# A 4096 x 4096 x 4096 matmul with leaky ReLU: casts, evictions and stores dealt out anew to the engines

## The chip, the cores and the metric

The kernel runs on one core of a Trainium2 chip. The metric is the device time of one execution in microseconds (us). The program is one launch; inputs and output lie in the chip's main memory (DRAM) in float32.

Engines as the profile names them: PE (TensorE, the matmuls), PEld (its weight loads), DVE (VectorE), ACT (ScalarE), POOL (GpSimd), SP (SyncE, which here only issues DMAs). An entry like ACTq or SPq is the part of an engine that issues DMAs and waits.

## What is computed

```python
a: (4096, 4096) float32     # m, k
b: (4096, 4096) float32     # k, n
alpha = 0.01
x = a @ b
out = where(x > 0, x, alpha * x)      # (4096, 4096) float32
```

Both inputs are random normal numbers. The kernel rounds a and b to bfloat16 and accumulates in float32.

## The kernel before, in words

**Tiles.** K is cut into `KU` = 4 units of 1024 (`KC` = 8 slices of 128). M is cut into `MB` = 4 blocks of 1024 rows, each with two halves (`h`) of 512 rows, that is `MT` = 4 row blocks (`mt`) of 128. N is cut into 4 column blocks of `RN` = 1024, that is `NP` = 2 pieces (`nt`) of 512. A *region* is one half of a block of rows times one column block: 512 x 1024 of the output. It fills all eight PSUM banks (4 row blocks x 2 pieces of 512 columns) and takes 4 units x 64 = 256 matmuls of 128 x 512. There are 32 regions (8192 matmuls), in this order: block of rows, column block (forwards in even blocks, backwards in odd ones), half. Two neighbouring regions share B (a *pair*), and at a change of the block of rows B stays as well, so there are 13 different pairs of B loads.

**A.** `load_a` (line 67) fetches a row block's 128 rows x 1024 k in four DMAs of SyncE (32 partitions each, runs of 1 KB, quarters in the order 0, 2, 1, 3) into one of four `a32` buffers, rounds them to bfloat16 on VectorE (line 74, a strided cast) and transposes 32 x 32 blocks on VectorE (line 76) into `at`. There are 10 `at` buffers, for 8 units in use.

**B.** `load_b` (line 81) fetches 128 x 1024 (512 KB) in one DMA of SyncE into one of four `b32` buffers and rounds it on ScalarE (line 84) into `bt`. There are 5 `bt` buffers of one unit.

**Order of the work.** The program is written out by hand (`manual_schedule`): each engine runs its instructions in the order in which the Python code issues them, and waits only by semaphores for data and for free buffers. `jobs` (lines 98 to 112) attaches the loads to units: a pair's B one region ahead, a new block's A two regions and a unit ahead. A unit's loads are issued before its matmuls (line 169). So all casts of a region's units stand on ScalarE ahead of that region's evictions.

**Start.** `first_unit` loads A's four row blocks and B's eight slices of one unit in the order `ababbabbabbb`. In region 0, the units 0 to 2 run their matmuls in the order in which those pieces arrive; unit 3, and all units of the later regions, run row block by row block (`mt`, then c, then `nt`). Region 1's A is loaded at the end of region 0.

**End of a region.** In unit 3, after each row block, ScalarE empties its two banks (line 196, leaky ReLU into an `o` tile of 128 x 512, four buffers) and issues the two stores itself (line 201, 256 KB each). The next region's first matmul on a bank waits for that.

Of the kernel before, what the change touches and what calls it, by code (L numbers as in the profile page):

```python
# [7 lines left out]
P = 128  # L8
BF16 = mybir.dt.bfloat16
FP32 = mybir.dt.float32  # L10
KC = 8
NT = 512
MT = 4
NP = 2


@with_exitstack
def kernel(
    ctx: ExitStack,
    tc: tile.TileContext,  # L20
    a: bass.AP,
    b: bass.AP,
    alpha,
    out: bass.AP,
):

    nc = tc.nc
    M, K = a.shape
    K2, N = b.shape
# [9 lines left out]
    QW = KC * P // 4  # L45

    a_v = a.rearrange("(mt g i) (u q w) -> mt u q i g w", g=4, i=32, q=4, w=QW)
    b_v = b.rearrange("(u p c) n -> u p c n", u=KU, p=P, c=KC)
# [12 lines left out]
    at = {}  # L61
    bt = {}

    def new_a(mb, h, u):
        at[mb, h, u] = at_pool.tile([P, KC, RM], BF16, name="at")

    def load_a(mb, h, u, mt):

        tile_no = (mb * HALVES + h) * MT + mt
        a32 = a32_pool.tile([P, 4, QW], FP32, name="a32")  # L70
        for q in (0, 2, 1, 3):
            nc.sync.dma_start(a32[32 * q:32 * q + 32], a_v[tile_no, u, q])  # L72
        a16 = a16_pool.tile([P, 4, KC, 32], BF16, name="a16")
        nc.vector.tensor_copy(a16, a32.rearrange("p g (j c) -> p g c j", c=KC))  # L74
        dst = at[mb, h, u][:, :, mt * P:(mt + 1) * P].rearrange("p c (g i) -> p g c i", g=4)
        nc.vector.transpose(dst, a16)  # L76

    def new_b(pair, n, u):
        bt[pair, u] = bt_pool.tile([P, KC, RN], BF16, name="bt")

    def load_b(pair, n, u, c):
        b32 = b32_pool.tile([P, RN], FP32, name="b32")
        nc.sync.dma_start(b32, b_v[u, :, c, n * RN:(n + 1) * RN])  # L83
        nc.scalar.copy(bt[pair, u][:, c, :], b32)  # L84


    regions = []
    pairs = []
    for mb in range(MB):
        order = list(range(NB)) if mb % 2 == 0 else list(range(NB - 1, -1, -1))  # L90
        for n in order:
# [6 lines left out]
    jobs = {}  # L98
    for s_region, (mb, h, pi, n) in enumerate(regions):
        if h:  # L100
            continue
        for u in range(KU):
            if regions[s_region - 1][2] != pi or s_region == 0:
                s = s_region * KU + u
                jobs.setdefault(max(0, s - KU), []).append(("b", pi, n, u, s))
            if s_region and regions[s_region - 1][0] != mb:
                for hh in range(HALVES):
                    idx = hh * KU + u
                    s = s_region * KU + idx
                    jobs.setdefault(s - HALVES * KU - 1, []).append(("a", mb, hh, u, s))  # L110

    jobs = {s: [j for j in v if not (j[0] == "b" and j[1] == 0)] for s, v in jobs.items()}

    def run(job):
        if job[0] == "a":
            _, mb, h, u, _ = job
            new_a(mb, h, u)
            for mt in range(MT):
                load_a(mb, h, u, mt)
        else:  # L120
            _, pi, n, u, _ = job
            new_b(pi, n, u)
            for c in range(KC):
                load_b(pi, n, u, c)


    w = warm_pool.tile([P, NT], BF16, name="w")
    nc.vector.memset(w, 0.0)  # L128
    wp = psum_pool.tile([P, NT], FP32, name="ps")
    for i in range(9):  # L130
        nc.tensor.matmul(wp, w[:, :P], w, start=True, stop=True)  # L131

    def first_unit(u):
        new_a(0, 0, u)
        new_b(0, 0, u)
        for what in "ababbabbabbb":
            if what == "a":
                load_a(0, 0, u, first_unit.a)
                first_unit.a += 1
            else:  # L140
                load_b(0, 0, u, first_unit.b)
                first_unit.b += 1
        first_unit.a = first_unit.b = 0

    first_unit.a = first_unit.b = 0

    def mm(ps, mb, h, pi, u, mt, nt, c):
        nc.tensor.matmul(  # L148
            ps,
            at[mb, h, u][:, c, mt * P:(mt + 1) * P],  # L150
            bt[pi, u][:, c, nt * NT:(nt + 1) * NT],
            start=(u == 0 and c == 0),
            stop=(u == KU - 1 and c == KC - 1),
        )

    first_unit(0)
    for r, (mb, h, pi, n) in enumerate(regions):
        banks = {}
        for u in range(KU):
            s = r * KU + u  # L160
            if r == 0:
                if u + 1 < KU:
                    first_unit(u + 1)
                else:
                    for uu in range(KU):
                        new_a(0, 1, uu)
                        for mt in range(MT):
                            load_a(0, 1, uu, mt)
            for job in jobs.get(s, []):
                run(job)  # L170
            if u == 0:
                for mt in range(MT):
                    for nt in range(NP):
                        banks[mt, nt] = psum_pool.tile([P, NT], FP32, name="ps")
            if r == 0 and u < KU - 1:

                na = nb = 0
                for what in "ababbabbabbb":
                    if what == "a":
                        todo = [(na, c) for c in range(nb)]  # L180
                        na += 1
                    else:
                        todo = [(mt, nb) for mt in range(na)]
                        nb += 1
                    for mt, c in todo:
                        for nt in range(NP):
                            mm(banks[mt, nt], mb, h, pi, u, mt, nt, c)
                continue
            for mt in range(MT):
                for c in range(KC):  # L190
                    for nt in range(NP):
                        mm(banks[mt, nt], mb, h, pi, u, mt, nt, c)
                if u == KU - 1:
                    for nt in range(NP):
                        o = o_pool.tile([P, NT], FP32, name="o")
                        nc.scalar.activation(  # L196
                            o, banks[mt, nt], mybir.ActivationFunctionType.Lrelu, alpha=alpha
                        )
                        row = ((mb * HALVES + h) * MT + mt) * P
                        col = n * RN + nt * NT  # L200
                        nc.scalar.dma_start(out[row:row + P, col:col + NT], o)  # L201


# [33 lines left out]
```

## Time and profile before

| What | Value |
|---|---|
| Median of 3 runs | 1885.15 us (1880.54 to 1890.42) |
| The profiled execution | 1889.55 us |
| Its span, first to last instruction | 1887.7 us |
| Mean granted TensorE clock | 0.973 |
| PE busy | 1797.8 us (95%), 8201 matmuls with 9 for warming up |
| ACT busy | 581.3 us (31%) |
| DVE busy | 293.0 us (16%) |
| DMA | 353.65 MB, mean 187 GB/s |

The span leaves out what lies around the first and the last instruction (1.85 us here). The profile gives, for each engine and group of instructions, busy time, the mean of one, and the idle time before it with its releaser: what ended the wait. A busy PE need not be PE at its full rate, since matmuls are pipelined; the granted clock and the number of matmuls in a stretch tell that. Times in the views are in us from the span's start.

### The profile page before, as it was taken

What the parts mean: (1) busy time and instruction counts of PE and PEld (TensorE: products, weight loads), DVE (VectorE), ACT (ScalarE), POOL (GpSimd) and SP (SyncE); (2) the same over time, 40 slices, a digit from 0 to 9 for tenths busy, and PEclk for the clock granted to TensorE, in tenths of its full rate; (3) what the DMA queues carried; (4) which work ended last, traced back from release to release, by engine and by line L of the source; (5) the groups of instructions that cost most, each with busy time, mean ns of one, the idle gap of its engine ahead of it and who ended that gap; (6) DMA issues with size and microseconds to landing.
All of it is one profiled execution on the core that took longest, in us unless ns stands there. A gap on an engine that the chain in (4) does not pass through costs nothing.

```text
span 1887.7 us, 19704 instructions
## 1 busy us (share of the span) xinstructions
PE 1797.8 (95%) x8201; PEld 806.5 (43%) x8201; DVE 293.0 (16%) x257; ACT 581.3 (31%) x674; POOL 0.2 (0%) x4
## 2 busy tenths in 40 slices
PE   6694999999999899999999989999999989999999
PEld 2241444444444344444444434444444434444444
DVE  4470000013341000004323000000434100000000
ACT  3316153351004426052111524426001260624411
POOL 0000000000000000000000000000000000000000
PEclk8797999999999999999999989999999989999999
DMA  9989275484347719177433935628445590836511
GB/s 275 276 242 333 76 255 191 148 297 117 107 139 255 274 69 329 52 279 232 140 116 105 332 130 201 245 92 299 136 128 154 197 321 34 296 128 218 184 45 45
DMA packets 170585, 353.65 MB, mean 187 GB/s; under 512 B 18944, under 2 KB 84480, under 8 KB 170496
## 3 DMA queue, kind: packets, MB, share of 16 engines
q1 hardware_dynamic: 133632, 285.27, 46.7%
q10 hardware_dynamic: 36864, 67.13, 9.5%
q8 instruction: 64, 1.05, 0.2%
q14 instruction: 25, 0.20, 0.0%
HBM read 285.21 MB, written 67.11 MB: 187 GB/s over the span
## 4 chain that ended last, share of the span: by engine, by line
PE 80%; DMA 15%; ACT 3%; SPq 1%; issue 0%; DVE 0%; ACTq 0%; DVEq 0%
PE ps L148 80%; DMA b<-in_b_dram 13%; ACT bt L84 2%; DMA a<-in_a_dram 2%; SPq L72 1%; DMA out_dram<-o 1%; ACT o L196 1%; SPq L83 0%; DVE a L74 0%; ACTq L201 0%; DVE at L76 0%; DVEq L74 0%; ACTq L196 0%
## 5 line engine op out<-in xcount | busy, mean ns | idle before, releaser
L148 PE MATMUL ps<-bt,at 128*128 128x512 bf16 x8192 | 1793.9, 382 | 84.4 <-ACT o L196 54.0
L148 PEld LDWEIGHTS <-at 128*128 128x128 bf16 x8192 | 805.3, 98 | 1073.3 <-issue 97.8
L84 ACT CAST bt<-b 128x1024 bf16<-128x1024 f32 x416 | 427.1, 1044 | 334.8 <-DMA b<-in_b_dram 273.9
L196 ACT ACTIVATE o<-ps 128x512 f32<-128x512 f32 x256 | 152.8, 597 | 968.1 <-PE ps L148 874.1
L74 DVE CAST a<-a 128x1024 bf16<-128x1024 f32 x128 | 137.5, 1075 | 1197.9 <-DMA a<-in_a_dram 1197.6
L76 DVE STREAM_TRANSPOSE at<-a 128x1024 bf16<-128x1024 bf16 x128 | 159.4, 1245 | 6.0
L131 PE MATMUL ps<-w 128*128 128x512 bf16 x9 | 3.9, 613 | 1.2 <-DVE w L128 1.2
L131 PEld LDWEIGHTS <-w 128*128 128x128 bf16 x9 | 1.2, 141 | 3.1 <-issue 1.9
L84 ACT ACT_TABLE_LOAD x1 | 1.3, 1283 | 0.7 <-PEq L218 0.7
L196 ACT ACT_TABLE_LOAD x1 | 1.3, 1283 | 0.0
L128 DVE MEMSET w<- 128x256 uint32 x1 | 0.3, 272 | 0.9 <-PEq L218 0.9
L218 POOL MEMSET const-uint8-127<- 128x1 uint8 x1 | 0.1, 102 | 0.0
L218 POOL MEMSET const-bfloat16-1.0<- 128x1 bf16 x1 | 0.1, 101 | 0.0
L218 POOL MEMSET const-float32-0.0<- 128x1 f32 x1 | 0.1, 98 | 0.2 <-issue 0.2
L218 POOL MEMSET const-float32-1.0<- 128x1 f32 x1 | 0.1, 98 | 0.0
## 6 DMA issues: line engine op xcount, KB each, us to landing
b<-in_b_dram SPq DMA_DIRECT2D x416, 512.0 KB, 5.2
a<-in_a_dram SPq DMA_DIRECT2D x512, 128.0 KB, 3.6
out_dram<-o ACTq DMA_DIRECT2D x256, 256.0 KB, 2.0
```

Source lines behind the costliest of these rows:

```text
L72: nc.sync.dma_start(a32[32 * q:32 * q + 32], a_v[tile_no, u, q])
L74: nc.vector.tensor_copy(a16, a32.rearrange("p g (j c) -> p g c j", c=KC))
L76: nc.vector.transpose(dst, a16)
L84: nc.scalar.copy(bt[pair, u][:, c, :], b32)
L128: nc.vector.memset(w, 0.0)
L131: nc.tensor.matmul(wp, w[:, :P], w, start=True, stop=True)
L148: nc.tensor.matmul(ps, at[mb, h, u][:, c, mt * P:(mt + 1) * P], bt[pi, u][:, c, nt * NT:(nt + 1) * NT], start=(u == 0 and c == 0), stop=(u ...
L196: nc.scalar.activation(o, banks[mt, nt], mybir.ActivationFunctionType.Lrelu, alpha=alpha)
L218: nc = _bacc.Bacc("TRN2", target_bir_lowering=False, num_devices=1)
```

## The change

**Casts.** VectorE rounds B too, for all pairs but the first. ScalarE (`scalar=True`) rounds the first pair's B and the A of region 1; the transposes are all VectorE's. From region 1's end on, ScalarE runs only the evictions.

**Stores.** GpSimd issues them, one of 128 x 1024 (512 KB) per row block, from two `o` buffers of that size in place of four of 128 x 512. In the very last region SyncE issues them, per 512 columns, and there unit 3 finishes one bank after the other.

**Loads.** SyncE issues all of them as before, with each part of a unit's loads written behind a row block's matmuls (`issue`, `ahead`) instead of ahead of the unit. A's quarters go in the order 0, 1, 2, 3. Region 2's B is placed 2 units ahead and all other B 4 units ahead; a new block's A starts one unit behind the unit whose buffer it takes. `at` has 8 buffers instead of 10, `bt` 6 instead of 5.

**First k unit.** Unit 0 is split into two halves of 512 k (`subs`), for every block: A's runs are then 512 bytes, its tiles 128 x 512, and a half has four slices of B instead of eight. In region 0 the first half runs in the order of arrival (`abababab`), the second half and the units 1 and 2 slice by slice over all four row blocks, and unit 3 row block by row block. Region 1 runs likewise: slice by slice, and unit 3 row block by row block.

**Small things.** ScalarE's activation table is loaded at the start by a small activation on the warm-up tile; there are 12 warm-up matmuls instead of 9. `TURNS` has one entry, so the code for partial sums (`part`) does nothing.

On ScalarE, behind the start, nothing is left between evictions. On SyncE the first loads stand like this before (quarter DMAs of 32 x 4 x 256, counted by `x4`):

```order
L72 DMA a_95<-in_a_dram 32x4x256 x4
L83 DMA b_103<-in_b_dram 128x1024
L72 DMA a_106<-in_a_dram 32x4x256 x4
L83 DMA b_114<-in_b_dram 128x1024
L83 DMA b_117<-in_b_dram 128x1024
L72 DMA a_120<-in_a_dram 32x4x256 x4
```

and in the changed kernel, where the four A tiles of the first half have 32 x 4 x 128 to a quarter:

```order
L82 DMA a_98<-in_a_dram 32x4x128 x4
L99 DMA b_107<-in_b_dram 128x1024
L82 DMA a_110<-in_a_dram 32x4x128 x4
L99 DMA b_118<-in_b_dram 128x1024
L82 DMA a_121<-in_a_dram 32x4x128 x4
L99 DMA b_129<-in_b_dram 128x1024
```

The third A tile now stands behind two pieces of B instead of three, and each A tile is half as large. Around the end of region 0, ScalarE has this in the changed kernel (L237 empties region 0's banks, L86 rounds region 1's A):

```order
L101 CAST bt<-b_558 128x1024
L237 ACTIVATE o<-ps 128x512 x2
L86 CAST a_587<-a_582 128x512
L237 ACTIVATE o<-ps 128x512 x2
L86 CAST a_615<-a_610 128x512
```

where before it had evictions and stores in turn:

```order
L84 CAST bt<-b_458 128x1024
L196 ACT_TABLE_LOAD
L196 ACTIVATE o<-ps 128x512
L201 DMA out_dram<-o 128x512
L196 ACTIVATE o<-ps 128x512
L201 DMA out_dram<-o 128x512
```

The stores have left ScalarE, and one cast of A stands behind each row block's two evictions.

The diff, cut to its core:

```diff
-    at_pool = ctx.enter_context(tc.tile_pool(name="at", bufs=HALVES * KU + 2))
-    bt_pool = ctx.enter_context(tc.tile_pool(name="bt", bufs=KU + 1))
+    subs = [(0, 0, 4, 0), (0, 4, 4, 512)] + [(u, 0, 8, 1024 * u) for u in range(1, KU)]
+    subs_of = {u: [s for s in subs if s[0] == u] for u in range(KU)}
+
+    at_pool = ctx.enter_context(tc.tile_pool(name="at", bufs=HALVES * KU))
+    bt_pool = ctx.enter_context(tc.tile_pool(name="bt", bufs=KU + 2))
...
-    o_pool = ctx.enter_context(tc.tile_pool(name="oo", bufs=4))
+    o_pool = ctx.enter_context(tc.tile_pool(name="oo", bufs=2))
...
-        for q in (0, 2, 1, 3):
-            nc.sync.dma_start(a32[32 * q:32 * q + 32], a_v[tile_no, u, q])
-        a16 = a16_pool.tile([P, 4, KC, 32], BF16, name="a16")
-        nc.vector.tensor_copy(a16, a32.rearrange("p g (j c) -> p g c j", c=KC))
+        u, c0, kc, k0 = sub
...
+        w = 32 * kc
+        a32 = a32_pool.tile([P, 4, w], FP32, name="a32")
+        for q in range(4):
+            src = a[row:row + P, k0 + q * w:k0 + (q + 1) * w]
+            nc.sync.dma_start(a32[32 * q:32 * q + 32], src.rearrange("(g i) w -> i g w", i=32))
+        a16 = a16_pool.tile([P, 4, kc, 32], BF16, name="a16")
+        a32_v = a32.rearrange("p g (j c) -> p g c j", c=kc)
+        if scalar:
+            nc.scalar.copy(a16, a32_v)
+        else:
+            nc.vector.tensor_copy(a16, a32_v)
...
-        nc.scalar.copy(bt[pair, u][:, c, :], b32)
+        if scalar:
+            nc.scalar.copy(bt[pi, u][:, c0 + c, :], b32)
+        else:
+            nc.vector.tensor_copy(bt[pi, u][:, c0 + c, :], b32)
...
+            lead = 2 if pi == 1 else KU
+            loads.setdefault(first * KU + u - lead, []).extend(pieces)
...
+                loads.setdefault(first * KU + h * KU + u - 2 * KU + 1, []).extend(pieces)
...
+        if h:
+            return [lambda mt=mt: load_a(0, 1, sub, mt, True) for mt in range(MT)]
+        order = "abababab" if sub[2] == 4 else "ababbabbabbb"
...
+            if t == len(TURNS) - 1:
+                o = o_pool.tile([P, RN], FP32, name="o")
+                for nt in range(NP):
+                    done = banks[mt, nt] if len(TURNS) == 1 else part[h][:, mt, nt, :]
+                    nc.scalar.activation(o[:, nt * NT:(nt + 1) * NT], done, LRELU, alpha=alpha)
+                nc.gpsimd.dma_start(place(0, h, pairs[0], mt), o)
...
+        elif last:
+            for mt in range(MT):
+                for c in range(kc):
+                    go(mt, c)
+                spill(mt)
+                ahead(mt)
+                if i >= extra:
+                    issue(2 * KU - 2 + i - extra, mt)
+        else:
+            for quarter in range(4):
+                for c in range(kc * quarter // 4, kc * (quarter + 1) // 4):
+                    for mt in range(MT):
+                        go(mt, c)
+                ahead(quarter)
...
-                if u == KU - 1:
-                    for nt in range(NP):
-                        o = o_pool.tile([P, NT], FP32, name="o")
-                        nc.scalar.activation(
-                            o, banks[mt, nt], mybir.ActivationFunctionType.Lrelu, alpha=alpha
-                        )
...
-                        nc.scalar.dma_start(out[row:row + P, col:col + NT], o)
+                if final and last:
+                    order = [(c, nt) for nt in range(NP) for c in range(KC)]
+                else:
+                    order = [(c, nt) for c in range(KC) for nt in range(NP)]
...
+                if last:
+                    o = o_pool.tile([P, RN], FP32, name="o")
...
+                        nc.scalar.activation(o[:, cols], banks[mt, nt], LRELU, alpha=alpha)
+                        if final:
+                            nc.sync.dma_start(to[:, cols], o[:, cols])
+                    if not final:
+                        nc.gpsimd.dma_start(to, o)
+                issue(r * KU + u, mt)
```

More of the change, by code (lines that the diff above doesn't have):

```diff
@@ L78, in new_b, with load_a @@
[L78 to L84 removed]
+    def load_a(mb, h, sub, mt, scalar=False):
+        u, c0, kc, k0 = sub
+        if (mb, h, u) not in at:
+            at[mb, h, u] = at_pool.tile([P, KC, RM], BF16, name="at")
+        row = ((mb * HALVES + h) * MT + mt) * P
+        w = 32 * kc
[9 more added lines that the diff above has]
+            nc.vector.tensor_copy(a16, a32_v)
+        dst = at[mb, h, u][:, c0:c0 + kc, mt * P:(mt + 1) * P]
+        nc.vector.transpose(dst.rearrange("p c (g i) -> p g c i", g=4), a16)
@@ new lines, in mm, with new_banks, place @@
+    def mm(ps, mb, h, pi, u, mt, nt, c, first, last):
+        nc.tensor.matmul(
+            ps,
+            at[mb, h, u][:, c, mt * P:(mt + 1) * P],
+            bt[pi, u][:, c, nt * NT:(nt + 1) * NT],
+            start=first,
+            stop=last,
+        )
+    def new_banks():
+        return {
+            (mt, nt): psum_pool.tile([P, NT], FP32, name="ps")
+            for mt in range(MT)
+            for nt in range(NP)
+        }
+    def place(mb, h, n, mt):
+        row = ((mb * HALVES + h) * MT + mt) * P
+        return out[row:row + P, n * RN:(n + 1) * RN]
@@ L87 @@
+    w = warm_pool.tile([P, NT], BF16, name="w")
+    nc.vector.memset(w, 0.0)
+    nc.scalar.activation(w[:, :8], w[:, :8], LRELU, alpha=alpha)
+    wp = psum_pool.tile([P, NT], FP32, name="ps")
+    for _ in range(12):
+        nc.tensor.matmul(wp, w[:, :P], w, start=True, stop=True)
     regions = []
@@ L89 @@
     for mb in range(MB):
-        order = list(range(NB)) if mb % 2 == 0 else list(range(NB - 1, -1, -1))
-        for n in order:
+        for n in range(NB) if mb % 2 == 0 else range(NB - 1, -1, -1):
             if not pairs or pairs[-1] != n:
@@ L112 @@
[L112 to L117, printed above, removed]
-            for mt in range(MT):
[L119 to L143, printed above, removed]
@@ new lines @@
+    loads = {}
+    for pi in range(1, len(pairs)):
+        first = next(i for i, r in enumerate(regions) if r[2] == pi)
+        for u in range(KU):
+            pieces = [
+                lambda pi=pi, sub=sub, c=c: load_b(pi, pairs[pi], sub, c)
+                for sub in subs_of[u]
+                for c in range(sub[2])
+            ]
+            lead = 2 if pi == 1 else KU
+            loads.setdefault(first * KU + u - lead, []).extend(pieces)
+    for mb in range(1, MB):
+        first = next(i for i, r in enumerate(regions) if r[0] == mb)
+        for h in range(HALVES):
+            for u in range(KU):
+                pieces = [
+                    lambda mb=mb, h=h, sub=sub, mt=mt: load_a(mb, h, sub, mt)
+                    for sub in subs_of[u]
+                    for mt in range(MT)
+                ]
+                loads.setdefault(first * KU + h * KU + u - 2 * KU + 1, []).extend(pieces)
@@ new lines, in issue, with step_loads @@
+    def issue(slot, part):
+        pieces = loads.get(slot, [])
+        for piece in pieces[len(pieces) * part // 4:len(pieces) * (part + 1) // 4]:
+            piece()
+    steps = [
+        (t, h, sub, i == len(turn) - 1)
+        for t, turn in enumerate(TURNS)
+        for h in range(HALVES)
+        for i, sub in enumerate(turn)
+    ]
+    def step_loads(t, h, si):
+        sub = subs[si]
+        if h:
+            return [lambda mt=mt: load_a(0, 1, sub, mt, True) for mt in range(MT)]
+        order = "abababab" if sub[2] == 4 else "ababbabbabbb"
+        made, na, nb = [], 0, 0
+        for what in order:
+            if what == "a":
+                made.append(lambda mt=na: load_a(0, 0, sub, mt))
+                na += 1
+            else:
+                made.append(lambda c=nb: load_b(0, pairs[0], sub, c, True))
+                nb += 1
+        return made
@@ new lines @@
+    for r in range(HALVES, len(regions)):
+        mb, h, pi, n = regions[r]
+        banks = new_banks()
+        final = r == len(regions) - 1
+        for u in range(KU):
+            last = u == KU - 1
+            for mt in range(MT):
+                if final and last:
+                    order = [(c, nt) for nt in range(NP) for c in range(KC)]
+                else:
+                    order = [(c, nt) for c in range(KC) for nt in range(NP)]
+                for c, nt in order:
+                    mm(banks[mt, nt], mb, h, pi, u, mt, nt, c, u == 0 and c == 0,
+                       last and c == KC - 1)
+                if last:
+                    o = o_pool.tile([P, RN], FP32, name="o")
+                    to = place(mb, h, n, mt)
+                    for nt in range(NP):
+                        cols = slice(nt * NT, (nt + 1) * NT)
+                        nc.scalar.activation(o[:, cols], banks[mt, nt], LRELU, alpha=alpha)
[4 more added lines that the diff above has]
+                issue(r * KU + u, mt)
```

127 lines of the change are left out of this document (61 added, 66 removed).

## The prediction

> **What bounds the kernel now.** First the page: who is busy, what the span holds.
>
> ```profile
> span 1887.7 us, 19704 instructions
> PE 1797.8 (95%) x8201; PEld 806.5 (43%) x8201; DVE 293.0 (16%) x257; ACT 581.3 (31%) x674; POOL 0.2 (0%) x4
> L148 PE MATMUL ps<-bt,at 128*128 128x512 bf16 x8192 | 1793.9, 382 | 84.4 <-ACT o L196 54.0
> ```
>
> The matmuls are the bound, so the question is how much of the span is not matmuls at full rate. That rate comes from a stretch without a gap, in the table by windows (columns: length, then busy time and count of PE, PEld, DVE, ACT, POOL, then the granted clock):
>
> ```profile
> 200.00:400.00 200.00, 200.00 (x928) 90.69 (x927) 0.00 (x0) 71.09 (x80) 0.00 (x0) 1.00 0.51 179
> ```
>
> 200/928 is 0.2155 us a matmul at clock 1.00; 8192 of them are 1765.4 us, and 122.3 us of the span are something else. The timeline of PE alone says where (start, length, count, idle ahead and what ended it):
>
> ```profile
> 93.37 67.94 PE L148 MATMUL ps<-bt,at 128*128 128x512 bf16 x306 [1.24 <-ACT bt L84]
> 189.79 0.58 PE L148 MATMUL ps<-bt,at 128*128 128x512 bf16 x1 [28.48 <-ACT o L196]
> 190.80 9.57 PE L148 MATMUL ps<-bt,at 128*128 128x512 bf16 x32 [0.43 <-ACT o L196]
> ...
> 199.78 435.50 PE L148 MATMUL ps<-bt,at 128*128 128x512 bf16 x2017
> 643.00 0.59 PE L148 MATMUL ps<-bt,at 128*128 128x512 bf16 x1 [7.72 <-ACT o L196]
> 644.01 443.16 PE L148 MATMUL ps<-bt,at 128*128 128x512 bf16 x2047 [0.43 <-ACT o L196]
> 1094.85 0.59 PE L148 MATMUL ps<-bt,at 128*128 128x512 bf16 x1 [7.68 <-ACT o L196]
> 1095.87 444.21 PE L148 MATMUL ps<-bt,at 128*128 128x512 bf16 x2047 [0.43 <-ACT o L196]
> 1548.52 0.59 PE L148 MATMUL ps<-bt,at 128*128 128x512 bf16 x1 [8.44 <-ACT o L196]
> 1549.53 333.85 PE L148 MATMUL ps<-bt,at 128*128 128x512 bf16 x1535 [0.43 <-ACT o L196]
> ```
>
> So there is a start-up of 93 us in which only some 200 matmuls run, four stops behind ScalarE, and nothing else. Next, what ScalarE did before the first stop, from the timeline of all engines:
>
> ```profile
> 134.64 54.95 SPq L83 DMA_DIRECT2D b<-in_b_dram  x36
> ...
> 188.20 1.04 ACT L84 CAST bt<-b 128x1024 bf16<-128x1024 f32 x1 [0.23 <-DMA b<-in_b_dram]
> 189.15 0.59 ACT L196 ACTIVATE o<-ps 128x512 f32<-128x512 f32 x1
> ```
>
> PE had filled all eight banks at 161.3, but ScalarE was rounding region 2's B, at the pace of its DMAs, until 189.2, and emptied nothing meanwhile. And why B came so late, from SyncE's waits (total, times, longest):
>
> ```profile
> SPq L83 <- DMA out_dram<-o: 403.6, 8, 51.3
> ```
>
> SyncE's loads wait for stores to land: in the program the issues of SyncE and ScalarE take turns on one set of semaphores, so loads stand behind stores, and stores behind evictions.
>
> **The change, part by part.** Sum against the profiled execution: span 1887.7, time 1889.55.
>
> *The four stops go.* On ScalarE, region 1's last stretch and region 2's B, before:
>
> ```order
> L84 CAST bt<-b_1030 128x1024
> L84 CAST bt<-b_1033 128x1024
> L84 CAST bt<-b_1036 128x1024
> L84 CAST bt<-b_1039 128x1024
> L84 CAST bt<-b_1042 128x1024
> L196 ACTIVATE o<-ps 128x512
> L201 DMA out_dram<-o 128x512
> ```
>
> and in the changed kernel (a_ are region 1's A pieces; the first `x8` empties region 1):
>
> ```order
> L86 CAST a_930<-a_925 128x1024
> L86 CAST a_961<-a_956 128x1024
> L86 CAST a_991<-a_986 128x1024
> L86 CAST a_1021<-a_1016 128x1024
> L237 ACTIVATE o<-ps 128x512 x8
> L294 ACTIVATE o<-ps 128x512 x240
> ```
>
> Region 2's 32 casts are gone from ahead of the evictions, and from there ScalarE has nothing but evictions. Ahead of region 1's evictions now stand casts of region 1's own A, which its matmuls need anyway. Idle removed: 28.48+7.72+7.68+8.44 and four times 0.43, 54.0. With it goes the slow stretch after each stop: 32+2017 matmuls took 445.1 instead of 441.6, 2047 took 443.2 and 444.2 instead of 441.1, 1535 took 333.9 instead of 330.8, and the four single ones 0.37 too much each: 3.5+2.1+3.1+3.1+1.5 = 13.3. **Minus 67.3.**
>
> What is late next? Region 2 would start near 163 and needs B unit by unit, 13.8 us apart. On VectorE, region 1's last A unit and region 2's first B unit stand now together (before, only A casts and transposes ran there):
>
> ```order
> L90 STREAM_TRANSPOSE at<-a_930 128x4x8x32
> L103 CAST bt<-b_934 128x1024
> L103 CAST bt<-b_937 128x1024
> L90 STREAM_TRANSPOSE at<-a_961 128x4x8x32
> L103 CAST bt<-b_964 128x1024
> L103 CAST bt<-b_967 128x1024
> ```
>
> Behind a blocked transpose stand two casts of B each, and behind those SyncE's next loads (four buffers); nothing of ScalarE's. Two views of the DMA, first A alone (112 to 134 us), then B alone (140 to 186), then start-up, give rates:
>
> ```profile
> DMA packets 5914, 5.41 MB, mean 246 GB/s; under 512 B 654, under 2 KB 5912, under 8 KB 5912
> ...
> DMA packets 4227, 15.42 MB, mean 335 GB/s; under 512 B 467, under 2 KB 467, under 8 KB 4226
> ...
> DMA packets 12450, 23.04 MB, mean 288 GB/s; under 512 B 1380, under 2 KB 8647, under 8 KB 12447
> ```
>
> One DMA issue of SyncE and the end of region 0's matmuls, from the chain of waits:
>
> ```profile
> 3.06 0.43 SPq L72
> ...
> 93.37 12.48 PE ps L148 x49
> ```
>
> Call that end T; it is 105.9 now. At 0.43 us an issue, four to a tile, region 1's A comes at 1.7 us a tile at best and is in by about T+38 together with B's first unit; three more units of 4.2 MB at 300 GB/s (between A's and B's rates) follow by T+52, T+66, T+80. Region 2 starts at T+57 and needs them at T+71, T+84 and T+98. Covered by 17 us or so.
>
> *Casts moved to VectorE.* 384 of B's casts. The rows:
>
> ```profile
> L84 ACT CAST bt<-b 128x1024 bf16<-128x1024 f32 x416 | 427.1, 1044 | 334.8 <-DMA b<-in_b_dram 273.9
> L196 ACT ACTIVATE o<-ps 128x512 f32<-128x512 f32 x256 | 152.8, 597 | 968.1 <-PE ps L148 874.1
> L74 DVE CAST a<-a 128x1024 bf16<-128x1024 f32 x128 | 137.5, 1075 | 1197.9 <-DMA a<-in_a_dram 1197.6
> L76 DVE STREAM_TRANSPOSE at<-a 128x1024 bf16<-128x1024 bf16 x128 | 159.4, 1245 | 6.0
> ```
>
> At 1.08 us (its strided cast) they add 413 us to 293: under 40% of the span. The fullest region of 55.2 us has 32 casts (34 us) or 16 A tiles (37 us). Hidden; cost 0. Without that cover each region would lose what goes over 55.2 us.
>
> *Stores on GpSimd, 512 KB each, two `o` buffers.* Not in the trace. Nearest rows, per issue:
>
> ```profile
> b<-in_b_dram SPq DMA_DIRECT2D x416, 512.0 KB, 5.2
> out_dram<-o ACTq DMA_DIRECT2D x256, 256.0 KB, 2.0
> ```
>
> A row block finishes every 16 matmuls, 3.45 us. The third needs the first one's buffer; its bank is wanted 20.7 us into a period that starts at u 3, and the first store is issued at about 4.7. With 1.2 us of eviction, a store may take 14.8 us before PE notices; the rows say 2 to 5. Cost 0. SyncE's loads no longer wait on stores, which helps what is hidden already.
>
> *First k unit in halves.* A's pieces of 512 bytes instead of 1 KB. From the rates, one of 16 engines spends 66.6 ns on 1 KB (16×1024/246) and 195.6 ns on 4 KB; the line through both gives 45.1 ns for 512 bytes, 182 GB/s. Region 0's 2.1 MB of such pieces then take 11.5 us instead of 8.5, on the path, since the start is all DMA. **Plus 3.0**; bounds 0 (bytes alone count) and 8.5 (packets alone count). The first matmuls come a little sooner, but region 0 cannot end before all 25.2 MB are in, and its last unit is still run block by block, so the 48 matmuls behind the last B cast stay.
>
> *The A quarters go out as 0, 1, 2, 3 instead of 0, 2, 1, 3.* No row shows the new order. In start-up B pieces over all partitions stand between A tiles, and 288 GB/s is near the mix of the two rates (8.4 MB at 246 and 16.8 MB at 335 would be 299); I take 0. Upper bound: A's worst slice in that window, 158 GB/s, would make its 34.1 us 53, plus 19.
>
> ```profile
> GB/s 88 199 259 270 270 237 251 263 238 233 255 253 266 266 246 283 259 266 255 158 218 248 263 240 255 253 242 265 242 196 281 279 225 291 263 263 212 257 266 263
> ```
>
> [...]
>
> *Region 0 to 1.* Region 1 now takes all four row blocks for each c, so after six matmuls (1.3 us) it wants block 3's bank and A. ScalarE first empties block 3 (two times 0.6, with a gap of 0.4: T+1.7), then casts its half A tile (0.6), then VectorE transposes (0.7): T+3.0. **Plus 1.7**, bounds 1.2 (no gap) and 2.7 (halves cost like wholes, rows above).
>
> *Tail.* The last block is finished bank by bank, so one eviction and its gap leave the end, where the chain shows both:
>
> ```profile
> 1883.20 0.61 ACT o L196
> 1883.83 0.34 ACTq L201
> 1884.27 0.60 ACT o L196
> ```
>
> **Minus 1.0.** Three more warm-up matmuls and the early table load lie in the wait for the first data: 0.
>
> Sum: −67.3+3.0+1.7−1.0 = −63.6: 1826 for the profiled execution. That one lies 4.4 above the median of the runs shown, so 1821.5 against the median 1885.15; the forecast is **1822**.
>
> **The rivals.** *Start-up costs more.* Small pieces at their upper bound (5.5 more) and half of the 19 us of the quarter order: 1837. For it: everything before 93 us is DMA. Against: B's pieces in between.
>
> *Stops at the block changes stay.* Each new block's A loses its two spare buffers, so its transposes wait for PE, with B's casts behind. If these three stops stay, 25.1 us of idle and 9.4 of slow stretch: 1856. Against: block A is allowed in two regions ahead, and B's casts come a region later.
>
> [...]
>
> *It doesn't do what it says.* The evictions are freed, but B's loads themselves set region 2's start: no change, 1885. Against: the 17 us above.
>
> **How the numbers follow.** Forecast 0.68, dear start 0.17, stops stay 0.06, stores 0.05, no change 0.03, and 0.01 for a start-up that gets shorter. A measurement here can tell about 0.5%, 9 us, from no change. Faster: 0.68+0.17+0.06+0.01 = 0.92; same 0.03; slower 0.05. The range holds the forecast with its bounds (3 less if small pieces are free; runs differ by 5 either way; 1.0 and 5.5 more at the upper ends) and the dear start: 1812 to 1843.
>
> **What would show it.** Right: after T, now about 109, PE is one row without idle over 2 us, 31 regions of 55.2; no PE wait on ScalarE; ScalarE near 200 us busy; SyncE never waits for a store; start-up still DMA-bound near 288 GB/s. Wrong: idle of PE near 161 or every eight regions, ScalarE waiting on stores, a start-up DMA rate under 270, or a granted clock below 1.00 in the middle.

## The result, and the profile after

The changed kernel takes 1836.15 us (median of 4 runs, 1834.01 to 1840.84) against 1882.97 us before (median of 4). The ratio is 0.9748, with a 95% interval of 0.9713 to 0.9783. The profiled execution took 1836.29 us, with a span of 1834.5 us at a granted clock of 0.988. So the change made the kernel 2.5% faster, where the forecast was 3.3% (1822 us); the time lies inside the range of 1812 to 1843, 14 us above the forecast.

From the page of the changed kernel, its first lines and the groups that answer to those of before:

```profile
span 1834.5 us, 19653 instructions
PE 1777.4 (97%) x8041; PEld 804.5 (44%) x8204; DVE 536.0 (29%) x685; ACT 207.0 (11%) x310; POOL 73.3 (4%) x128
L103 DVE CAST bt<-b 128x1024 bf16<-128x1024 f32 x384 | 256.9, 692 | 876.1 <-PE ps L106 575.3
L298 POOL DMA_DIRECT2D out_dram<-o x116 | 68.2, 588 | 1531.8 <-ACT o L294 1526.3
L86 ACT CAST a<-a 128x1024 bf16<-128x1024 f32 (+1 forms) x20 | 33.1, 1673 | 19.8 <-DMA a<-in_a_dram 19.7
out_dram<-o POOLq DMA_DIRECT2D x124, 512.0 KB, 3.4
```

ScalarE fell from 581 to 207 us, VectorE rose from 293 to 536, and a store from GpSimd lands 3.4 us after its issue. Some matmul records are missing here (8041 of 8204), as the weight loads show; the stretches below are read by their lengths. PE's timeline in the changed kernel, from the last two B casts of region 0 to the end (the view lists gaps down to about 0.2 us):

```profile
99.14 1.01 PE L106 MATMUL ps<-bt,at 128*128 128x512 bf16 x2 [0.72 <-ACT bt L101]
100.58 14.28 PE L106 MATMUL ps<-bt,at 128*128 128x512 bf16 x55 [0.43 <-ACT bt L101]
116.30 13.55 PE L106 MATMUL ps<-bt,at 128*128 128x512 bf16 x61 [1.44 <-DVE at L90]
130.81 0.60 PE L106 MATMUL ps<-bt,at 128*128 128x512 bf16 x2 [0.95 <-DVE at L90]
133.00 1697.92 PE L106 MATMUL ps<-bt,at 128*128 128x512 bf16 x7709 [1.59 <-DVE at L90]
```

All four stops are gone: after 133.0 us PE runs in one row to its last matmul. What is left is the start, which became longer (the last stretch of region 0 began at 100.58 us instead of 93.37), and three new short waits in region 1, all for VectorE's transposes of A. The waits of ScalarE and PE say the same (total, times, longest):

```profile
ACT o L294 <- DMA out_dram<-o: 69.5, 21, 5.1
...
PE ps L106 <- DVE at L90: 29.6, 10, 5.6
...
PE ps L106 <- ACT bt L101: 12.9, 8, 3.1
```

PE waits nowhere for an eviction any more. ScalarE does wait for GpSimd's stores, up to 5.1 us at a time, and PE never sees it. The prediction had named that wait as a sign of being wrong; here it costs nothing. Another of its signs, a start-up DMA rate under 270 GB/s, is only just missed (271 from 30 to 90 us, below).

### The profile page after: what moved, and what is told of

Its sections match the earlier page's. It is cut to its first block, busy times and chain, and to the rows that moved or that the text cites. A ratio compares the mean times of both kernels' runs of the same rounds, so it can differ in the third digit from the quotient of the medians.

```text
span 1834.5 us, 19653 instructions
## 1 busy us (share of the span) xinstructions
PE 1777.4 (97%) x8041; PEld 804.5 (44%) x8204; DVE 536.0 (29%) x685; ACT 207.0 (11%) x310; POOL 73.3 (4%) x128
## 3 DMA queue, kind: packets, MB, share of 16 engines
q8 instruction: 64, 1.05, 0.2%
## 4 chain that ended last, share of the span: by engine, by line
PE 93%; DMA 5%; ACT 1%; issue 1%; SPq 0%; DVE 0%; ACTq 0%
PE ps L106 93%; DMA b<-in_b_dram 4%; DMA a<-in_a_dram 1%; SPq L82 0%; ACT bt L101 0%; ACT a L86 0%; DVE at L90 0%; ACT o L294 0%; SPq L99 0%; ACT o L237 0%; ACTq L86 0%; ACTq L237 0%
## 5 line engine op out<-in xcount | busy, mean ns | idle before, releaser
L106 PE MATMUL ps<-bt,at 128*128 128x512 bf16 x8029 | 1772.9, 381 | 51.2 <-DVE at L90 29.6
L103 DVE CAST bt<-b 128x1024 bf16<-128x1024 f32 x384 | 256.9, 692 | 876.1 <-PE ps L106 575.3
L294 ACT ACTIVATE o<-ps 128x512 f32<-128x512 f32 x240 | 130.7, 595 | 1524.5 <-PE ps L106 1386.7
L90 DVE STREAM_TRANSPOSE at<-a 128x1024 bf16<-128x1024 bf16 (+1 forms) x160 | 165.1, 1032 | 218.3 <-PE ps L106 141.4
L88 DVE CAST a<-a 128x1024 bf16<-128x1024 f32 (+1 forms) x140 | 122.2, 873 | 70.8 <-DMA a<-in_a_dram 70.8
L298 POOL DMA_DIRECT2D out_dram<-o x116 | 68.2, 588 | 1531.8 <-ACT o L294 1526.3
L101 ACT CAST bt<-b 128x1024 bf16<-128x1024 f32 x32 | 33.5, 1046 | 64.8 <-DMA b<-in_b_dram 64.8
L86 ACT CAST a<-a 128x1024 bf16<-128x1024 f32 (+1 forms) x20 | 33.1, 1673 | 19.8 <-DMA a<-in_a_dram 19.7
L238 POOL DMA_DIRECT2D out_dram<-o x8 | 4.9, 608 | 172.1 <-ACT o L237 172.1
L237 ACT ACTIVATE o<-ps 128x512 f32<-128x512 f32 x16 | 8.7, 597 | 14.7 <-PE ps L106 8.9
```

Of the source, the lines that this page charges most:

```text
L86: nc.scalar.copy(a16, a32_v)
L88: nc.vector.tensor_copy(a16, a32_v)
L90: nc.vector.transpose(dst.rearrange("p c (g i) -> p g c i", g=4), a16)
L101: nc.scalar.copy(bt[pi, u][:, c0 + c, :], b32)
L103: nc.vector.tensor_copy(bt[pi, u][:, c0 + c, :], b32)
L106: nc.tensor.matmul(ps, at[mb, h, u][:, c, mt * P:(mt + 1) * P], bt[pi, u][:, c, nt * NT:(nt + 1) * NT], start=first, stop=last,)
```

## The experiments

**The start and region 1: four kernels.** First, the quarters of A in the old order.

```diff
-        for q in range(4):
+        for q in (0, 2, 1, 3):
```

> The changed kernel with A's four quarters issued as 0, 2, 1, 3 again. In the changed kernel the last B cast of region 0 ended at 100.5 us, in the kernel before at 93.3. Theory Q (neighbouring quarters slow A's loads): the DMA rate of 30 to 92 us goes from 270 back to 286 GB/s, the last cast comes 3.5 to 4.5 us earlier, near 96.5, and the time falls by about 4 us (ratio to before about 0.9725). Rival P (the 512-byte pieces of the first unit cost all of it): last cast stays at 100.5 within 1 us, time unchanged.

Measured: 1835.22 us, ratio 0.9732 (0.9709 to 0.9756). PE's row at the last B cast of region 0:

```profile
96.54 14.08 PE L106 MATMUL ps<-bt,at 128*128 128x512 bf16 x55 [0.28 <-ACT bt L101]
```

The DMA view of 30 to 90 us, in the changed kernel and then in this one:

```profile
DMA packets 8957, 16.27 MB, mean 271 GB/s; under 512 B 993, under 2 KB 6322, under 8 KB 8954
```

```profile
DMA packets 9571, 17.56 MB, mean 293 GB/s; under 512 B 1062, under 2 KB 6699, under 8 KB 9568
```

PE resumed 4.0 us earlier after the last cast and the rate rose, as theory Q said. The time moved by too little to tell from no change. Second, the first unit whole.

```diff
-    subs = [(0, 0, 4, 0), (0, 4, 4, 512)] + [(u, 0, 8, 1024 * u) for u in range(1, KU)]
+    subs = [(u, 0, 8, 1024 * u) for u in range(KU)]
-TURNS = [[0, 1, 2, 3, 4]]
+TURNS = [[0, 1, 2, 3]]
...
-            for c in range(kc):
-                for mt in range(c):
-                    go(mt, c)
-                for cc in range(c + 1):
-                    go(c, cc)
+            na = nb = 0
+            for what in "ababbabbabbb":
+                if what == "a":
+                    todo = [(na, c) for c in range(nb)]
+                    na += 1
+                else:
+                    todo = [(mt, nb) for mt in range(na)]
+                    nb += 1
+                for mt, c in todo:
+                    go(mt, c)
```

> The changed kernel with the first k unit whole again (A in pieces of 1 KB, arrival order of the kernel before in region 0's first unit), quarters as changed. Theory Q: only the 2 to 3 us that the first 26 us lost come back, last cast near 98. Rival P: nearly all of the 7.2 us comes back, last cast near 94, time down by 6 to 7 us. Beside it both expect region 1's waits to move, since its first unit is then one step of whole tiles.

Measured: 1831.83 us, ratio 0.9719 (0.9695 to 0.9744).

```profile
95.39 13.91 PE L106 MATMUL ps<-bt,at 128*128 128x512 bf16 x55 [0.19 <-ACT bt L101]
112.12 1713.42 PE L106 MATMUL ps<-bt,at 128*128 128x512 bf16 x7772 [2.83 <-DVE at L90]
```

That is 5.2 us earlier, nearer to rival P. In region 1 one wait of 2.83 us stands in place of three. Third, both of these undone (the two diffs together).

> The changed kernel with both undone: first unit whole and quarters 0, 2, 1, 3. Both theories expect the last B cast at 93.3 to 94.5, that is the start-up of the kernel before, and a time 6 to 8 us under the changed kernel. If the last cast stays near 97 or later, something else in the start is slow (the order of matmuls, buffers, waits of SyncE).

Measured: 1832.34 us, ratio 0.9722 (0.9696 to 0.9748), and the row stands at 95.84:

```profile
95.84 14.89 PE L106 MATMUL ps<-bt,at 128*128 128x512 bf16 x55 [1.33 <-ACT bt L101]
113.56 1713.42 PE L106 MATMUL ps<-bt,at 128*128 128x512 bf16 x7772 [2.83 <-DVE at L90]
```

So undoing both brought no more than undoing the first unit alone, and less than either theory asked. One profile of the start cannot divide 7 us between two causes; how far it varies, the later runs show. Fourth, region 1's A rounded on VectorE.

```diff
-            return [lambda mt=mt: load_a(0, 1, sub, mt, True) for mt in range(MT)]
+            return [lambda mt=mt: load_a(0, 1, sub, mt) for mt in range(MT)]
```

> The changed kernel with region 1's A rounded on VectorE instead of ScalarE. Theory (ScalarE's strided cast, 2.05 us a tile against 1.06 on VectorE, is what makes region 1's A late): PE's waits near 116, 131 and 133 us (1.4, 1.0 and 1.6 us) shrink to under 1.5 us in all, time down by 2 to 4 us. Rival (SyncE's issue of four DMAs a tile, 1.7 us, sets the pace): the waits stay at 3 us or more and the time does not move.

Measured: 1832.61 us, ratio 0.9728 (0.9704 to 0.9753).

```profile
104.23 1726.12 PE L106 MATMUL ps<-bt,at 128*128 128x512 bf16 x7827 [0.24 <-ACT bt L101]
```

From the last B cast to the end PE is one row: all three waits of region 1 came from having these casts on ScalarE, and SyncE's issue does not set the pace. How much of that is ScalarE's strided cast (2.05 us a tile) and how much the place behind region 0's evictions, this run does not separate. Its start, with the same loads as the changed kernel's, ended 3.6 us later than there in the profiled execution, which eats the gain there (1835.70 us against 1836.29).

**Which part removed the stops: four kernels.** The casts alone, in the kernel before:

```diff
-        nc.scalar.copy(bt[pair, u][:, c, :], b32)
+        if pair == 0:
+            nc.scalar.copy(bt[pair, u][:, c, :], b32)
+        else:
+            nc.vector.tensor_copy(bt[pair, u][:, c, :], b32)
```

> The kernel before with one part of the change alone: B's casts on VectorE for all pairs but the first. Stores stay on ScalarE. Theory (the evictions stand behind casts in ScalarE's queue, and that alone makes the four stops): all four stops go, 50 to 65 us less, about 1820 to 1833. Rival (the loads that wait for stores are the cause): a stop near 161 us stays, now behind B itself, at 10 us or more, and those at the block changes at 3 us or more; gain under 35 us.

Measured: 1840.24 us against 1886.71, ratio 0.9743 (0.9714 to 0.9772). PE's rows from the last B cast of region 0 on:

```profile
97.16 63.77 PE L151 MATMUL ps<-bt,at 128*128 128x512 bf16 x290 [0.63 <-ACT bt L85]
163.10 6.61 PE L151 MATMUL ps<-bt,at 128*128 128x512 bf16 x22 [2.18 <-DVE at L76]
172.77 0.59 PE L151 MATMUL ps<-bt,at 128*128 128x512 bf16 x2 [3.06 <-DVE bt L87]
...
179.11 1655.74 PE L151 MATMUL ps<-bt,at 128*128 128x512 bf16 x7666 [0.40 <-DVE bt L87]
```

No wait for an eviction is left and the stops at the block changes are gone. Yet between 161 and 179 us PE waits 8.2 us in six pieces, 6.1 of it directly for region 2's B and 2.2 for the last A tile of region 1. The gain, 46.5 us, is less than the 50 to 65 expected and more than the rival's 35. The theory of the queue explains most of it, the rival a rest. Then the stores alone:

```diff
-                        nc.scalar.dma_start(out[row:row + P, col:col + NT], o)
+                        nc.gpsimd.dma_start(out[row:row + P, col:col + NT], o)
```

> The kernel before with the other part alone: the 256 KB stores issued by GpSimd, so that SyncE's loads no longer wait for them. B's casts stay on ScalarE, ahead of the evictions. Theory of the queue: the stop at region 2 stays at 15 to 25 us (B comes some 7 us earlier), the stops at the block changes shrink; gain 10 to 35 us. Rival of the shared semaphores: all four stops shrink to under 3 us, gain 50 us or more.

Measured: 1853.07 us, ratio 0.9816 (0.9788 to 0.9844).

```profile
99.11 67.44 PE L148 MATMUL ps<-bt,at 128*128 128x512 bf16 x306 [0.68 <-ACT bt L84]
184.34 1660.76 PE L148 MATMUL ps<-bt,at 128*128 128x512 bf16 x7680 [17.79 <-ACT o L196]
```

The stop at region 2 stays, with 17.8 us instead of 28.5, and the other three are gone here too. At the first block change ScalarE's last cast and first evictions stand 16 us earlier than in the kernel before. There, and then here:

```profile
641.40 1.04 ACT L84 CAST bt<-b 128x1024 bf16<-128x1024 f32 x1 [0.76 <-DMA b<-in_b_dram]
642.35 0.59 ACT L196 ACTIVATE o<-ps 128x512 f32<-128x512 f32 x1
```

```profile
625.10 1.04 ACT L84 CAST bt<-b 128x1024 bf16<-128x1024 f32 x1 [0.73 <-DMA b<-in_b_dram]
626.05 2.05 ACT L196 ACTIVATE o<-ps 128x512 f32<-128x512 f32 x4
```

At the block changes either part is enough; at region 2 only moving the casts removes the stop. Both together, in the kernel before:

> The kernel before with both parts, and nothing else of the change (old pools, old load order, whole units, old quarter order). Theory of the queue: as the casts alone, within 5 us; start-up as before (last B cast near 93.3), so 1818 to 1828, which is below the changed kernel's 1836. Rival: only both together free the loads, 20 us or more below the casts alone.

Measured: 1828.37 us, ratio 0.9682 (0.9652 to 0.9713).

```profile
98.82 1724.98 PE L151 MATMUL ps<-bt,at 128*128 128x512 bf16 x7986 [0.67 <-ACT bt L85]
```

One row from the last B cast on. These two edits alone do all that the change does for the stops, and the interval ends where that of the changed kernel begins. The time is 11.9 us below that of the casts alone: more than the 5 of the theory, less than the 20 of its rival. Last, the changed kernel with its stores on ScalarE again:

```diff
-                nc.gpsimd.dma_start(place(0, h, pairs[0], mt), o)
+                nc.scalar.dma_start(place(0, h, pairs[0], mt), o)
...
-                        nc.gpsimd.dma_start(to, o)
+                        nc.scalar.dma_start(to, o)
```

> The changed kernel with the 512 KB stores issued by ScalarE again, so that SyncE's loads wait for them. Theory of the queue: no change within 5 us, since VectorE casts and evictions are still on time, though SyncE shows waits for stores. Rival of the shared semaphores: stops come back near region 2 or at the block changes, 10 us or more slower. [...]

Measured: 1840.65 us, ratio 0.9751 (0.9727 to 0.9775), the same as the changed kernel's. PE's last row and, from SyncE's waits, the two rows on loads that waited for stores:

```profile
138.11 1697.92 PE L106 MATMUL ps<-bt,at 128*128 128x512 bf16 x7866 [1.85 <-DVE at L90]
```

```profile
SPq L82 <- DMA out_dram<-o: 261.8, 40, 27.3
...
SPq L99 <- DMA out_dram<-o: 81.7, 14, 15.1
```

SyncE's loads of A and B wait 343 us for stores again, and no stop comes back: with the new order of loads there is room for it. Nor is it faster, so GpSimd's way of storing costs nothing that shows; this start ended 3.6 us later than the changed kernel's (104.2 against 100.6), which is within its spread.

**The loads by themselves.** A probe of the start's loads:

```python
kinds = ["wold", "wnew", "hnew", "hold", "hold", "hnew", "wnew", "wold"]
for i, kind in enumerate(kinds):          # w: 1 KB pieces, h: 512 bytes; old: 0, 2, 1, 3; new: 0, 1, 2, 3
    for half in range(2):
        ...                               # one unit of A and B with load_a and load_b, no matmul
```

> A probe with no matmuls, whose output is left almost wholly unwritten: the start-up's loads, casts and transposes by themselves. Sixteen units of A and B in region 0's mixed order, two units each of: whole units with quarters 0, 2, 1, 3 (wold), whole with 0, 1, 2, 3 (wnew), halves with 0, 1, 2, 3 (hnew), halves with 0, 2, 1, 3 (hold), and the same backwards; then A alone in 1 KB pieces, 16 tiles each of old, new, new, old order (xold, xnew). [...] Theory P: halves take 2 to 3 us a unit more with either order, and the order alone under 0.5 us. [...]

SyncE's timeline, the first issue of each stretch (the first number is its time, the name of the tile after `DMA_DIRECT2D` tells the kind; `hold` ran four units in a row, the others two):

```profile
0.73 1.80 SPq L59 DMA_DIRECT2D awold<-in_a_dram  x4
...
41.48 1.75 SPq L59 DMA_DIRECT2D awnew<-in_a_dram  x4
...
85.22 2.22 SPq L59 DMA_DIRECT2D ahnew<-in_a_dram  x4
...
134.91 2.21 SPq L59 DMA_DIRECT2D ahold<-in_a_dram  x4
...
224.38 2.96 SPq L59 DMA_DIRECT2D ahnew<-in_a_dram  x4
...
271.85 1.78 SPq L59 DMA_DIRECT2D awnew<-in_a_dram  x4
...
317.51 2.21 SPq L59 DMA_DIRECT2D awold<-in_a_dram  x4
...
363.59 37.01 SPq L59 DMA_DIRECT2D axold<-in_a_dram  x64
```

| A unit of 6.3 MB | each time, us | mean, us |
|---|---|---|
| whole, old order | 20.4, 23.0 | 21.7 |
| whole, new order | 21.9, 22.8 | 22.4 |
| halves, old order | 22.4 | 22.4 |
| halves, new order | 24.8, 23.7 | 24.3 |

These are times from first issue to first issue. The issues run ahead of the data: the last B cast of a stretch ended 4.8 to 8.5 us after the next stretch's first issue. So the first stretch, which began with empty buffers, comes out short. From the end of a stretch's last B cast to the end of the next one's, a unit took 22.2 us (whole, old order), 22.0 and 23.8 (whole, new order), 22.7 (halves, old) and 23.1 and 23.8 (halves, new); the first stretch has no such time.

Halves in the new order, which is what the changed kernel's first unit has, are the slowest by either measure, by 2.6 us a unit over whole units in the old order in the table and by 1.3 from cast to cast. But one kind differs between its two times by up to 2.6 and 1.8, so the probe shows at most the sign and settles no size; the start-ups of the kernels themselves, below, do better. A alone, in both orders one after the other, does not tell the orders apart either:

```profile
363.60:473.00 109.40, 100.92 (x92) 4.12 (x4) 0.00 (x0) 1.00 1.09 235
```

The line has the length, busy time and count of VectorE, ScalarE and GpSimd, then the clock, the share of the DMA engines and GB/s. VectorE is busy 100.9 of 109.4 us with casts and transposes, and from 375 us on it never waits for a DMA. So it sets the pace with either order, although the DMA engines show as busy too. From 405 to 470 us, with the new order alone, A came at 232 GB/s.

**All three undone.** The diffs of the first, second and fourth experiment in one kernel:

> The changed kernel with three things undone: first unit whole, quarters 0, 2, 1, 3, region 1's A rounded on VectorE. If the causes named are right: last B cast of region 0 near 97 (the start-up of the kernel before has been seen at 93.3 to 99.1 in five profiles), under 1.5 us of waits of PE after that, ratio to before 0.968 to 0.970, about 1825 us, that is 9 to 12 us under the changed kernel. If the run stays above 0.972, part of the miss lies elsewhere, in what the kernel before loses from run to run.

Measured: 1822.2 us, ratio 0.9658 (0.9632 to 0.9684), better than the 0.968 to 0.970 expected. This is the lowest time of all kernels here; its interval lies below the changed kernel's and overlaps that of the two edits in the kernel before.

```profile
91.81 1725.03 PE L106 MATMUL ps<-bt,at 128*128 128x512 bf16 x7986 [0.41 <-ACT bt L101]
```

PE waits for nothing after the last B cast, as expected. That cast came 5 us earlier than expected, with the same loads as in the third experiment (95.84): the DMA moved 316 GB/s here from 4 to 16 us and 279 there, and no edit accounts for that. So a part of this time is a fast start.

**The two kernels once more.**

> The kernel before once more, for a second profile of its start and its stops. If its start-up is as variable as the experiments suggest, the last B cast of region 0 ends between 93 and 100 us, not at 93.3 again; the four stops are there, the one at region 2 at 20 to 30 us and those at the block changes at 7 to 9.

The kernel before again: 1888.06 us, and PE's rows are

```profile
97.14 68.22 PE L148 MATMUL ps<-bt,at 128*128 128x512 bf16 x306 [0.20 <-ACT bt L84]
193.31 0.58 PE L148 MATMUL ps<-bt,at 128*128 128x512 bf16 x1 [27.95 <-ACT o L196]
```

with 6.66, 7.47 and 6.23 us at the block changes (7 to 9 were expected).

> The changed kernel once more. Three profiles with its start-up code ended the last B cast of region 0 at 100.5, 104.2 and 104.2 us; expected 100 to 105 again, and three waits of PE in region 1 of 3 to 5 us together, then none. If the last cast comes before 98, the start-up's cost of the change is noise.

The changed kernel again: 1834.85 us, and

```profile
99.92 13.58 PE L106 MATMUL ps<-bt,at 128*128 128x512 bf16 x56 [0.21 <-ACT bt L101]
114.94 13.55 PE L106 MATMUL ps<-bt,at 128*128 128x512 bf16 x62 [1.44 <-DVE at L90]
129.33 0.61 PE L106 MATMUL ps<-bt,at 128*128 128x512 bf16 x2 [0.83 <-DVE at L90]
131.58 1697.92 PE L106 MATMUL ps<-bt,at 128*128 128x512 bf16 x7866 [1.65 <-DVE at L90]
```

Now the start can be judged. PE resumed after the last B cast of region 0 at 93.4, 97.2, 99.1, 98.8 and 97.1 us in the five profiles with the start-up code of the kernel before (mean 97.1), and at 100.6, 104.2, 104.2 and 99.9 in the four with the changed kernel's (mean 102.2); with only the loads of before put back, at 95.8 and 91.8. With one of the two put back it was 96.5 (quarters) and 95.4 (first unit). The change costs the start some 5.1 us, and single profiles lie up to 4 us off their mean. ScalarE's 32 casts of B in region 0 tell in which units (from ScalarE's timelines: when the eighth, the last of the first unit, ended, and how much later the 32nd ended):

| Start-up loads | eighth cast ended at, us | the other 24 took, us |
|---|---|---|
| of the kernel before (five profiles) | 27.2 to 29.6, mean 28.2 | 66.1 to 71.3, mean 68.9 |
| of the changed kernel (four) | 29.0 to 31.2, mean 30.3 | 69.8 to 73.8, mean 71.9 |
| quarters put back (one) | 30.3 | 66.2 |
| first unit put back (one) | 24.6 | 70.7 |
| both put back (two) | 27.0, 24.0 | 68.8, 67.8 |

The first unit is 2.1 us later in the changed kernel, and stays so with the quarters put back, which speaks for the halves as its cause. The other three units, whose loads differ from before only in the quarters' order, take 3.0 us more, and 1.8 more with the first unit put back. Over all profiles these three units take 68.4 us in the old order (eight) and 71.6 in the new (five). The whole first unit in the changed kernel ended earlier still, at 24.0 to 27.0, so the halves may cost up to 5 us there; one of these three profiles is the fast start of the kernel with three things undone.

## Why the prediction was right, and where its sizes were off

**The stops.** Right. All four went, PE waits for no eviction, and from region 1's second unit on it runs as one row. The slower matmuls behind the stops went too: 7866 took 0.2159 us each (at a granted clock of 1.00 from 133 to 1800 us), where the 2047 behind a stop before had taken 0.2165 and 0.2170 each. The mechanism held with one correction: the prediction put all four on evictions behind casts. At region 2 that is so (with the stores alone moved, 17.8 us stay). At the block changes moving the stores was enough as well, so there the casts were late because SyncE's loads had waited for stores.

**"Region 2's B is covered by 17 us or so."** No wait came there, even when the changed kernel's stores went back to ScalarE, but the cover was only 5.5 to 10 us. Region 2 began at 173.1 us (186 matmuls after 133.0) and wanted a unit every 13.8; VectorE's casts of its four units of B ended at 167.6, 180.4, 193.2 and 204.6. Counted from T, the end of region 0's matmuls, that is 11 to 16 us later than the prediction had them. With the old order of loads and the casts alone moved the cover was not there: 8.2 us of waits. The stores' part of the change, costed at nothing, is worth that much under the old order.

**The casts on VectorE at cost 0.** Right, with room: 0.69 us a cast instead of the 1.08 assumed.

**The stores on GpSimd at cost 0.** Right. 3.4 us from issue to landing against 14.8 allowed. The 0.05 that the forecast left for a slower kernel by the stores was the author's estimate. The trace does show store issues that last longer beside a cast of VectorE, at a small price. VectorE's and GpSimd's rows in the changed kernel's timeline:

```profile
1048.21 0.69 DVE L103 CAST bt<-b 128x1024 bf16<-128x1024 f32 x1 [2.11 <-DMA b<-in_b_dram]
1048.26 0.76 POOL L298 DMA_DIRECT2D out_dram<-o  x1 [44.36 <-ACT o L294]
...
1051.71 0.53 POOL L298 DMA_DIRECT2D out_dram<-o  x1 [2.69 <-ACT o L294]
```

The first issue began 0.05 us after a cast did, lasted 0.76 us and ended 0.12 us after it; the second began between casts and lasted 0.53. So it is throughout: of the 116 issues 20 lasted longer than 0.55, up to 1.13, and each of these ended 0.11 to 0.13 us after a cast that it overlapped. Six lay within a transpose and lasted 0.53. The price is at most 0.6 us a store (1.13 against 0.53), and a store's 3.4 us leave 11.4 of the 14.8.

**First k unit in halves, plus 3.0.** The size of this one is about right: the first unit came 2.1 us later, with up to 5 possible. The price behind it was not sound: the 246 GB/s of A alone was read as the DMA's rate, but VectorE was busy 20.9 of those 22 us, and in the probe it set the pace of the same kind of loads.

**The quarters' order at 0.** Too low. The start as a whole costs 5.1 us instead of 3.0, and the three units in which only the order of the loads is new take 3.0 of it. In the probe A alone came at 232 GB/s in the new order, with VectorE setting the pace; why the order costs time no run shows.

**The base of the start.** The profile of before had the earliest start of five, 93.4 against a mean of 97.1. That was luck of one trace, and by it T was put at 108.9. In the profiled execution of the changed kernel it was 113.6 (100.58 plus 14.28 less six matmuls of region 1): 4.7 late, for the base and the order together.

**Region 0 to 1, plus 1.7.** Mis-sized: the waits are 1.44, 0.95 and 1.59, 4.0 in all. The sum had only the first of them, and that came out near its 1.7, although the half A tile's cast was put at 0.6: A's strided cast takes ScalarE 1.1 us for a half and 2.05 for a whole tile. The other two are for unit 1's A, which came late as well and stood in no term. With these casts on VectorE all three waits vanished.

**The rate.** 0.2155 us came from a count in 200 us. Over the changed kernel's 7866 matmuls in one row it is 1697.9/7866 = 0.2159, which is 2.6 us more over the 7680 from region 2 on, to which the sum applied it.

**Tail, minus 1.0.** Nearly: from PE's last matmul to the end of the span it is 3.6 us instead of 4.3.

**From the profiled execution to the median.** The sum took 4.4 us off because before's profiled execution was above its median. The changed kernel's was at its median (1836.29 against 1836.15), so this step was wrong by about 4.

Together 4.7+2.3+2.6+0.3+4 = 13.9 of the 14 us between 1822 and 1836. Two agreements of numbers are chance. The rival of a dear start named 1837, next to the time measured, but its sum needed 15 us more in the start, where 4.7 came. And the 1822.2 us of the kernel with three things undone is the forecast's number without the costs that the forecast had put in for them, with a fast start besides.

## What to carry to other kernels

Here an engine that both empties PSUM and works on arriving data stopped the matmuls when that data was late; giving the evictions an engine without DMA waits ahead of them was worth most (46.5 us alone), and loads that wait for stores made much of the lateness (33.6 us gone with the stores alone moved). Before a rate from a trace is used as the price of a transfer, look which engine was busy in the same window: where the consumer is busy in 20.9 of 22 us, as VectorE here, the rate may be the consumer's and not the DMA's. Price a cast by a row with the same access pattern on the same engine, and take a start-up from more than one profile.

## What the runs showed of the hardware

In the changed kernel's profile ScalarE rounded 128 x 1024 float32 in 1.05 us where it read in order and in 2.05 us where it read every eighth element; VectorE took 0.69 us and 1.06 us for the same two. In the same profile, each of the 20 store issues on GpSimd that took longer than 0.55 us overlapped one of VectorE's casts and ended 0.11 to 0.13 us after it; the six that lay within a transpose took 0.53 us. PE resumed after the same start-up loads at 93.4 to 99.1 us in five profiles of one code, with a DMA share of 1.07 from 30 to 90 us in the first of them, so a few microseconds of such a start are not the kernel's.
